# One layer of attention, RWKV-7 and PEER experts on one core: which token blocks gather their experts' rows, and which pair is retrieved jointly

## The chip, the cores and the metric

The kernel runs on one core of a Trainium2 chip. The metric is the device time of one execution, in microseconds. Engines are called TensorE (PE in the rows; PEld are its weight loads), VectorE (DVE), ScalarE (ACT), GpSimd (POOL) and SyncE (SP). SP issues the plain transfers, POOL the gathers.

## The reference

For 512 tokens of width 1024, in float32, the layer computes an input projection, eight heads of latent attention with a block-causal mask, eight heads of RWKV-7 time mixing (a recurrence over the tokens), an output projection with residual, and a PEER layer over 16384 experts. Only the last part is touched by the change. In short:

```python
h = rms_norm(x, g_ffn)
q = (h @ w_pq).reshape(TOK_BLOCK, 8, 2, 128)
s = einsum('thpd,hpnd->thpn', q, sub_keys)          # 8 heads, 2 halves, 128 keys each
s1, i1 = top_k(s[:, :, 0], 16); s2, i2 = top_k(s[:, :, 1], 16)
top_s, pos = top_k(all sums s1 + s2, 16)            # 16 experts per head: 128 per token
idx = i1 * 128 + i2 of these;  gate = softmax(top_s)
act = gelu(einsum('thkd,td->thk', expert_u[idx], h))
x = x + einsum('thk,thkd->td', gate * act, expert_v[idx])
```

## The kernel before, in words

The 512 tokens are four blocks (0 to 3) of 128. Each block goes through stages: F (front, norm and input projection), R (chunks, the parallel part of RWKV), M (latent, attention), S (scan, the recurrence, which needs S of the block before) and B (back). B holds the output projection (`out_proj`, L792), the norm (`norm_ffn`), the retrieval (`retrieve`: queries by L848, scores by L855, the best 16 by `top16`, L825 to L835, all on VectorE) and the route (`route`: the best 16 of the sums, and the experts' indices, L925). A block's S ends with its output `yT` (L782).

The program is unrolled. A loop at the end of the function writes the stages' pieces in the order in which they would run side by side, by costs given per stage; five lanes (R, M, S, B, late F) share buffers and banks within a lane. `BACK` says in which items the lane of B goes through the blocks: there (0), then (1, 2) jointly, then (3). A joint item streams the weights once for two blocks, with matmuls of 256 columns in the queries instead of 128. The tile framework then orders the instructions of each engine when the program is built: an instruction that stands earlier in the text goes first where two are ready, and a later one may run as soon as its inputs and buffers are there. Each engine works its own list off in order.

The experts of a block are computed in one of two ways:

- `GATHERED` blocks (`experts`, L969 to L996): for each of the 128 experts of a token, GpSimd issues an indirect DMA that fetches one 4 KB row of `expert_u` per partition (L978) into one of `GA` = 4 buffers `ga`; VectorE multiplies it with the token and sums (L988), and ScalarE takes the gelu by groups of 32. Then the same for `expert_v`, whose rows VectorE adds up in `acc` (L991). That is 256 gathers and 256 VectorE instructions per block; the groups of v of one stand between those of u of the next group.
- `DENSE` blocks (`dense`): their 256 tokens go through all 16384 experts, 128 to a tile. `up(e)` (L1103 as float32, or L1117 as three exact products of parts that ScalarE and VectorE split off, L1063 and L1064) gives activations. `gate_half` gives the gates, in 32 steps of eight tokens for each half of the experts: VectorE makes B (L1035, L1036), ScalarE makes A (eight instructions L1039 and one L1040), TensorE multiplies (L1043), ScalarE stores (L1048). `down(e)` multiplies activations with gates (L1134) and adds up the output in PSUM (L1138 as float32, L1149 in parts). At most 16 tiles of activations wait on chip and 12 more in DRAM, so 28 run before the first step down, which needs the gates of all tokens.

The dense part's tokens come from DRAM (`h2d`), written by `norm_ffn` of the dense blocks; a gathered block's `norm_ffn` transposes back and stores `h2r` instead. Block 1's first projections are kept in two of the buffers `ga`, which are idle then (`EARLY`).

The lines at the change are these, before:

```python
BACK = [("F", (0,)), ("F", (1,)), ("B", (0,)), ("B", (1, 2)), ("B", (3,))]
GATHERED = (0, 3)
DENSE = (1, 2)
...
    early.close()
    dense()
    for b in GATHERED:
        experts(b, *routed[b])
```

Of the kernel before, what the change touches and what calls it, by code (L numbers as in the profile page):

```python
# [29 lines left out]
TOPK = 16  # L30
# [4 lines left out]

# columns of the packed per-channel vectors
CV = {}
# [5 lines left out]
NCV = _n  # L43
# columns of the packed per-feature rows
RV = {}
# [4 lines left out]
NRV = _n  # L50
# candidate pairs (a, b) of the two sorted lists that can be among the best 16 sums, in order of a * 16 + b:
# (a, b) has (a + 1) * (b + 1) - 1 pairs before it that are at least as large
RUNS = [(a, TOPK // (a + 1)) for a in range(TOPK)]
NCAND = sum(n for _, n in RUNS)

# lanes of stages: buffers, banks and weight tiles (count, width) of each
LANE = {"R": 1, "M": 2, "S": 4, "F": 3, "B": 3}
# [4 lines left out]
PM = 7  # L62
BACK = [("F", (0,)), ("F", (1,)), ("B", (0,)), ("B", (1, 2)), ("B", (3,))]
# blocks whose tokens gather their experts' rows, blocks that go through all experts
GATHERED = (0, 3)
DENSE = (1, 2)
EARLY = 1
GROUP, GA = 32, 4
# dense blocks: gates of HALF * 128 experts at a time, in GBUFS tiles of SUB * 128; activations run AHEAD tiles ahead,
# FIRST of them before the first gates, KEPT more wait in DRAM  # L70
HALF, SUB, GBUFS = 64, 16, 5
FIRST, AHEAD, KEPT = 12, 16, 12
# [4 lines left out]
def u_whole(e):  # L77
    """float32 products of four passes, where the vector engine has no time to split; else three exact parts"""
    return e < 28 or 47 <= e - AHEAD < 64
# [7 lines left out]
def layer_kernel(ctx: ExitStack, tc: tile.TileContext, x, pos, cvec, rvec, w_mla, w_rwkv, w_uq, w_ukv, lora, g2,  # L87
# [4 lines left out]
    dp = ctx.enter_context(tc.tile_pool(name="dp", bufs=1, space=bass.MemoryType.DRAM))  # L92
    # what the last block's tail needs lies apart: its pools outlive those of the other stages
    pools, psums = {}, {}
    last = ctx.enter_context(ExitStack())
    pools[3] = last.enter_context(tc.tile_pool(name="wb", bufs=1, side="right"))
    psums[3] = last.enter_context(tc.tile_pool(name="psb", bufs=1, space=PSUM, side="right"))
    # the tail takes over the buffers of the second lane
    pools[2] = ctx.enter_context(tc.tile_pool(name="wm", bufs=1))
# [10 lines left out]
    lane = [3]  # L110
# [28 lines left out]

    # ---------------------------------------------------------------- constants  # L140
    def load_x(b):
# [55 lines left out]
    for b in LEVELS:  # L197
# [7 lines left out]
        lmask[b] = m  # L205
    # rows (beta s | kappa s), columns (alpha t | rho t)
    mmask = cst([P, 2, C], "mmask")
# [50 lines left out]

    # rotary tables, token-major
    posi = cst([P, NB], "posi", I32)  # L260
# [12 lines left out]
    for i, ph in ((0, 0.25), (1, 0.0)):  # L273
# [3 lines left out]
        src = ang  # L277
        for c in TWO_PI:
            V.scalar_tensor_tensor(red, kr, -c, src, op0=OP.mult, op1=OP.add)
            src = red  # L280
# [29 lines left out]
    def square_sum(src, scr, acc):  # L310
        """the squares go to a tile that is written after them"""
        act(scr, src, AF.Square, accum_out=acc)

    def head_squares(src, n, acc, h0=0):
        """acc[:, h0 + i] = sum of squares of src[:, i, :n]"""
        for i in range(src.shape[1]):
            act(sb([P, QK], "hscr", dt=BF16)[:, :n], src[:, i, :], AF.Square, accum_out=acc[:, h0 + i:h0 + i + 1])

    # ---------------------------------------------------------------- stages
    def norm_in(xt, hT, carry):  # L320
        """channel-major normalized tokens, after the last one of the block before"""
        ss = sb([P, 1], "ss", 2)
        square_sum(xt.rearrange("p (a b) -> p a b", a=KC), hT[:, :, 1:], ss)
        r = rstd(ss, 1, 1.0 / D, EPS, "nx")
        act(xt, xt, AF.Copy, scale=r)
        if carry is None:
            V.memset(hT[:, :, 0:1], 0.0)
        else:
            V.tensor_copy(hT[:, :, 0:1], carry)
        for i in range(2):  # L330
            p = bank()
            for j in range(4):
                nc.tensor.transpose(p[:, j * P:(j + 1) * P], xt[:, (4 * i + j) * P:(4 * i + j + 1) * P], ident)
            for j in range(4):
                act(hT[:, 4 * i + j, 1:P + 1], p[:, j * P:(j + 1) * P], AF.Copy, scale=col("g_mix", 4 * i + j))
            yield
        carry = sb([P, KC, 1], "carry", 2)
        V.tensor_copy(carry, hT[:, :, P:P + 1])
        return carry

    def rwkv_in(b, hT):
        pm = {}
        if b == EARLY:
            # the gather's buffers are idle until the first block's experts are known
            t = [gb([P, D], "ga", GA).rearrange("p (a b) -> p a b", b=P) for _ in range(2)]
            pm = {"k": t[0][:, 0:4], "r": t[0][:, 4:8], "v": t[1][:, 0:4], "x": t[1][:, 4:6]}
        for g, cols in (("x", (12, 13)), ("k", range(4, 8)), ("r", range(4)), ("v", range(8, 12))):
            if b != EARLY:
                pm[g] = sb([P, 4, P], "pm", PM, pool=wa) if len(cols) == 4 else sb([P, 2, P], "px", 2, pool=wa)
            for i, c in enumerate(cols):  # L350
                w = wtile(w_rwkv[c])
                p = bank()
                for kc in range(KC):
                    mm(p[:, :P + 1], w[:, kc, :], hT[:, kc, :], start=kc == 0, stop=kc == KC - 1)
                t = pm[g][:, i, :]
                act(t, p[:, 1:P + 1], AF.Copy, scale=ommu[:, c:c + 1])
                V.scalar_tensor_tensor(t, p[:, 0:P], col("mu", c), t, op0=OP.mult, op1=OP.add)
                yield
        return pm

    def mla(b, hT, yT):
# [30 lines left out]
        yield  # L392
        # queries
        qs = sb([P, H], "qs")
# [30 lines left out]
        yield  # L425
        # keys and values
        kps, vps = bank(), bank()
# [24 lines left out]
        if b + 1 < NB:  # L452
            nc.sync.dma_start(vd[b], vb)
        # block-causal attention, four heads at a time
        nk = (b + 1) * P
# [72 lines left out]
    def rwkv_chunks(b, pm):  # L528
# [67 lines left out]
        yield  # L596
        # bonus weight and gate
        rk = r
# [6 lines left out]
        yield  # L605
        # values, token-major
        UV = [med(H, C) for _ in range(2)]
# [15 lines left out]
        yield  # L623
        # chunk-local products
        MT, BKt = [], []
        for c in range(2):
# [9 lines left out]
            yield  # L636
        # inverse of the unit lower triangular systems: two chunks stacked on the partitions, heads side by side
        for s in range(2):
# [15 lines left out]
        for c in range(2):  # L654
# [3 lines left out]
            t = med(4, P)  # L658
# [49 lines left out]
    def rwkv_scan(b, AR, BKt, MT, UV, YF, wc, bv, sg, yT):  # L708
        # the recurrence over chunks
        yt = med(H, C)  # L710
        for c in range(2):
# [4 lines left out]
            rows = slice(c * C, (c + 1) * C)  # L716
# [40 lines left out]
            yield  # L757
        # group norm, bonus, gate
        mean = sb([P, H], "mean")
# [64 lines left out]
    def top16(items):  # L824
        """items: (values, indices, source); the chains of several items interleaved"""  # L825
        for (v, i, src) in items:
# [10 lines left out]
    def retrieve(bs, h2T):  # L837
        """the best TOPK of both halves' keys, per block"""
        nb = len(bs)
# [22 lines left out]
    def route(b, tv, ti):  # L862
        yield
        # the lists of indices as steps: what each rank adds to the one before
        tf = ti.bitcast(F32)
# [11 lines left out]
        a = 0  # L877
        while a < TOPK:
            n = RUNS[a][1]
# [13 lines left out]
        for g in range(2):  # L893
            top16([(top[:, h], pi[:, h], cs_[:, h]) for h in range(4 * g, 4 * g + 4)])
            yield
        # rank a of the first list from a candidate's place, rank b of the second from its place within the run
        pf = pi.bitcast(F32)
# [40 lines left out]
        for i, (src, sc) in enumerate(ranks):  # L938
            if b in DENSE:
                summed(p[:, i * P:(i + 1) * P], stepped(src), sc, True)  # L940
            else:
                n = TOPK
# [85 lines left out]
    def gate_half(dn, g, parts):  # L1028
        """gates of experts i1 * 128 + i2, i1 in one half: [i2, sub, token, i1 of the SUB]; parts: what takes each run
        of subs"""  # L1030
        i1T, i2T, gT = slots
# [20 lines left out]
    def dense():  # L1052
# [8 lines left out]
        def split(t, hi, lo):  # L1061
            """two parts of a float32 tile that the one-pass products carry whole"""
            act(hi, t, AF.Copy)  # L1063
            V.tensor_tensor(lo, t, hi, op=OP.subtract)  # L1064
# [10 lines left out]
        hs = []  # L1075
        # room for activations in the buffers of the second lane
        room = [("q", 1, 3), ("k", 1, 3)] + [("wst", WST[2][0], 3)] * WST[2][0]
# [13 lines left out]
        def up(e, keep=False):  # L1091
            """activations of the experts of a tile, for all tokens of these blocks"""
            if e in kept:
# [89 lines left out]

    # stages of the blocks, emitted in the order in which they would run side by side; what runs in one lane shares
    # its buffers
    stages = {"F": (front, 16, 32), "R": (chunks, 24, 110), "M": (latent, 46, 95), "S": (scan, 10, 28),
# [10 lines left out]
    while any(lanes):  # L1197
# [19 lines left out]
        try:  # L1217
# [5 lines left out]
            lanes[i].pop(0)  # L1223
            running[i] = None
    early.close()
    dense()
    for b in GATHERED:
        experts(b, *routed[b])

# [57 lines left out]
```

## Time and profile before

| | us |
|---|---|
| median of 3 runs | 1783.02 |
| lowest, highest | 1781.82, 1790.86 |
| span of the profiled execution, first to last instruction | 1781.3 |
| TensorE matmul / weight load busy | 1651.5 / 1394.3 |
| VectorE / ScalarE / GpSimd busy | 1334.4 / 932.6 / 702.6 |
| mean granted TensorE clock | 0.950 |

The profile is of one execution. It gives the span and no other time for it; its span lies 1.7 us under the median of the runs. Busy times are unions of an engine's instructions; a matmul's end is modelled, and successive matmuls overlap in it. L12 is line 12 of the kernel. "out<-in" names what an instruction writes and reads, "x" counts the instructions of a group.

### The profile page before, as it was taken

The page shows a single profiled execution, that of the slowest core. Times are in us where ns is not written, and L with a number is a line of the kernel's source. Part 1 is how long each engine was busy: PE and PEld are TensorE (multiplying, and loading weights), DVE is VectorE, ACT ScalarE, POOL GpSimd, SP SyncE. Part 2 cuts the span into 40 slices and gives each one's busy share as a digit, 9 for nine tenths or more (in the row PEclk, how much of TensorE's full clock was granted, in tenths as well). Part 3 has the DMA queues.
Part 4 walks back from the last instruction along what each step waited for, and adds up shares of the span by engine and source line. Part 5 has one row for each costly group of instructions (what it writes and reads, how often), then busy time and mean ns, then how long its engine had stood idle before and what let it go on. Part 6 is the DMA issues. An engine that isn't in the chain of part 4 may idle for free. (4 is left out here: it accounts for less than half of the span.)

```text
span 1781.3 us, 29137 instructions
## 1 busy us (share of the span) xinstructions
PE 1651.5 (93%) x10183; PEld 1394.3 (78%) x10183; DVE 1334.4 (75%) x2987; ACT 932.6 (52%) x2465; POOL 702.6 (39%) x562
## 2 busy tenths in 40 slices
PE   7999999998999998788997899999999999999987
PEld 6897799787867987567995577888777778888864
DVE  3412414775586789887789789998887799999898
ACT  5656454644545332367774334444768645445443
POOL 1001100244554444454443253334455446356453
PEclk9998999997697999988999999999989999999999
DMA  7634565596689988789997799998989999999988
GB/s 272 196 122 135 164 233 194 203 337 223 213 309 329 324 321 294 290 283 310 364 331 250 258 359 352 359 355 325 327 312 319 312 343 351 366 318 371 346 293 330
DMA packets 154866, 520.71 MB, mean 292 GB/s; under 512 B 17312, under 2 KB 24096, under 8 KB 154720
## 3 DMA queue, kind: packets, MB, share of 16 engines
q0 software_dynamic: 73728, 268.47, 43.1%
q1 hardware_dynamic: 80992, 250.39, 39.6%
q8 instruction: 80, 1.31, 0.3%
q14 instruction: 66, 0.54, 0.1%
HBM read 508.96 MB, written 9.83 MB: 291 GB/s over the span
## 5 line engine op out<-in xcount | busy, mean ns | idle before, releaser
L978 POOL DMA_INDIRECT ga<-in_expert_v_dram,idx x256 | 352.3, 1376 | 381.7 <-DVE acc L991 285.5
L978 POOL DMA_INDIRECT ga<-in_expert_u_dram,idx x256 | 299.8, 1171 | 372.0 <-DVE ga L988 257.5
L991 DVE SCALAR_TENSOR_TENSOR acc<-ga,dots,acc 128x1024 f32<-128x1024 f32 x256 | 327.9, 1281 | 65.9 <-DMA ga<-in_expert_v_dram,idx 64.9
L988 DVE SCALAR_TENSOR_TENSOR ga<-ga,h 128x1024 f32<-128x1024 f32 x256 | 311.6, 1220 | 52.3 <-DMA ga<-in_expert_u_dram,idx 52.1
L1149 PE MATMUL po<-xh,t 128*128 128x512 f32 x880 | 307.7, 407 | 12.7 <-DVE t L1064 5.7
L1117 PE MATMUL ps<-dh,ul 128*128 128x256 f32 x664 | 191.1, 288 | 7.9 <-DVE ul L1064 7.4
L1149 PEld LDWEIGHTS po<-xh,t 128*128 128x128 f32 x880 | 159.6, 192 | 48.6 <-ACT xh L1063 13.2
L1117 PE MATMUL ps<-dh,uh 128*128 128x256 f32 x664 | 189.8, 286 | 6.5 <-ACT uh L1063 6.5
L1149 PE MATMUL po<-xl,t 128*128 128x512 f32 x440 | 179.6, 408 | 14.6 <-DVE xl L1064 14.2
L1117 PE MATMUL ps<-dl,uh 128*128 128x256 f32 x664 | 187.5, 282 | 0.0
L1063 ACT ACTIVATE xh<-v 128x512 fp32r<-128x512 f32 x220 | 134.6, 626 | 96.4 <-PE po L1149 73.9
L1103 PE MATMUL ps<-t,u 128*128 128x256 f32 x720 | 172.6, 393 | 9.1 <-DMA u<-in_expert_ut_dram 8.8
L1103 PEld LDWEIGHTS ps<-t,u 128*128 128x128 f32 x720 | 138.5, 197 | 32.3 <-issue 6.3
L1064 DVE TENSOR_TENSOR xl<-v,xh 128x512 fp32r<-128x512 f32 x220 | 147.7, 690 | 16.2 <-ACT xh L1063 15.7
L1043 PEld LDWEIGHTS ps<-B,A 128*128 128x128 f32 x1024 | 131.3, 204 | 35.3 <-ACT ge L951 10.6
L1039 ACT ACTIVATE A<-iotap,slots 128x128 f32<-128x128 f32 x512 | 156.1, 395 | 0.0
L1043 PE MATMUL ps<-B,A 128*128 128x64 f32 x1024 | 131.5, 285 | 23.6 <-DVE B L1036 10.4
L1063 ACT ACTIVATE uh<-u 128x512 fp32r<-128x512 f32 x166 | 98.5, 625 | 83.8 <-PE ps L1117 52.0
L1117 PEld LDWEIGHTS ps<-dh,ul 128*128 128x128 f32 x664 | 126.4, 190 | 17.3 <-DVE ul L1064 13.4
L1117 PEld LDWEIGHTS ps<-dh,uh 128*128 128x128 f32 x664 | 126.4, 190 | 17.1 <-ACT uh L1063 10.0
L1117 PEld LDWEIGHTS ps<-dl,uh 128*128 128x128 f32 x664 | 126.4, 190 | 3.5 <-issue 0.7
L848 PE MATMUL ps<-h2T,wst 128*128 128x128 f32 (+1 forms) x768 | 125.1, 318 | 3.1 <-DMA wst<-in_w_pq_dram 3.1
(402 smaller groups left out, 2924.1 us busy)
## 6 DMA issues: line engine op xcount, KB each, us to landing
u<-in_expert_ut_dram SPq DMA_DIRECT2D x128, 512.0 KB, 6.7
v<-in_expert_v_dram SPq DMA_DIRECT2D x128, 512.0 KB, 6.6
wst<-in_w_rwkv_dram SPq DMA_DIRECT2D x56, 512.0 KB, 4.4
wst<-in_w_pq_dram SPq DMA_DIRECT2D x48, 512.0 KB, 6.7
wst<-in_w_o_dram SPq DMA_DIRECT2D x24, 512.0 KB, 5.2
wst<-in_w_mla_dram SPq DMA_DIRECT2D x16, 336.0 KB, 3.9
t<-in_x_dram SPq DMA_DIRECT2D x8, 512.0 KB, 4.6
wst<-in_w_ukv_dram SPq DMA_DIRECT2D x16, 256.0 KB, 3.5
```

Of the source, the lines that this page charges most:

```text
L848: mm(p[:, :nb * P], w[:, kc, :], h2T[:, kc, :], start=kc == 0, stop=kc == KC - 1)
L978: G.indirect_dma_start(out=t, out_offset=None, in_=table, in_offset=bass.IndirectOffsetOnAxis(ap=idx[:, j:j + 1], axis=0))
L988: V.scalar_tensor_tensor(u, u, 1.0, h2, op0=OP.mult, op1=OP.mult, accum_out=dots[:, j:j + 1])
L991: V.scalar_tensor_tensor(acc, row_of(expert_v, j), dots[:, j:j + 1], acc, op0=OP.mult, op1=OP.add)
L1039: act(A[:, j, :], iotap, AF.Abs, scale=-1.0, bias=i2T[:, t0 + j:t0 + j + 1])
L1043: mm(p[:, j * HALF:(j + 1) * HALF], A[:, j, :], B[:, j, :], start=True, stop=True)
L1063: act(hi, t, AF.Copy)
L1064: V.tensor_tensor(lo, t, hi, op=OP.subtract)
L1103: mm(p, u[:, kc, :], hd[kc // 2][:, kc % 2, :], start=kc == 0, stop=kc == KC - 1)
L1117: mm(p, a[:, k, :], h[:, kc, :], start=kc + i == 0, stop=kc == KC - 1 and i == 2)
L1149: mm(po[i][n], ww[:, i * P:(i + 1) * P], vv, start=e + k == 0, stop=e == P - 1 and k == 2)
```

## The change

Blocks 0 and 1 gather, blocks 2 and 3 go through all experts. The lane of B goes through (0), (1) and then (2, 3) jointly. The gathered blocks' `experts` stand before `dense` in the text, and before the buffers of the early stages are released. The diff also takes comments out, which is left away here.

```diff
-BACK = [("F", (0,)), ("F", (1,)), ("B", (0,)), ("B", (1, 2)), ("B", (3,))]
+BACK = [("F", (0,)), ("F", (1,)), ("B", (0,)), ("B", (1,)), ("B", (2, 3))]
...
-GATHERED = (0, 3)
-DENSE = (1, 2)
+GATHERED = (0, 1)
+DENSE = (2, 3)
...
+    for b in GATHERED:
+        experts(b, *routed[b])
     early.close()
     dense()
-    for b in GATHERED:
-        experts(b, *routed[b])
```

## Rows read from the trace of the kernel before

**Rows 1.** The page: busy us, share of the span and instructions by engine.

```profile
PE 1651.5 (93%) x10183; PEld 1394.3 (78%) x10183; DVE 1334.4 (75%) x2987; ACT 932.6 (52%) x2465; POOL 702.6 (39%) x562
```

**Rows 2.** One line's instructions, L782, 600 to 800: ns min/median/max, first and last start.

```profile
L782 DVE TENSOR_TENSOR yT<-t,ps x1: 689/689/689, 733.7 to 733.7; 128x512 f32<-128x512 f32 x1
```

**Rows 3.** Busy us by stretch: length, PE, PEld, DVE, ACT, POOL, clock, DMA share, GB/s.

```profile
0.00:484.00 484.00, 461.30 (x3366) 400.19 (x3366) 215.04 (x716) 264.31 (x829) 97.84 (x91) 0.93 0.63 207
484.00:734.00 250.00, 232.12 (x1309) 190.42 (x1308) 197.03 (x585) 100.08 (x293) 122.43 (x107) 0.92 0.90 314
734.00:957.00 223.00, 197.67 (x1242) 173.00 (x1239) 189.59 (x532) 154.84 (x408) 96.17 (x83) 0.92 0.89 316
957.00:1781.00 824.00, 760.38 (x4273) 630.67 (x4271) 732.79 (x1159) 413.35 (x938) 386.15 (x282) 0.98 0.91 329
```

**Rows 4.** The gathers, L978: by line; POOL in 439:539; groups in 957:1781 (idle, releasers).

```profile
L978 POOL DMA_INDIRECT ga<-in_expert_u_dram,idx x256: 933/1086/3800, 338.7 to 1676.2; - x128
L978 POOL DMA_INDIRECT ga<-in_expert_v_dram,idx x256: 932/1152/6302, 433.9 to 1766.6; - x128
...
439.00:539.00 100.00, 44.73 (x39) 0.78 0.77 261
...
L978 POOL DMA_INDIRECT ga<-in_expert_v_dram,idx x154 | 234.3, 1522 | 228.3 <-DVE acc L991 191.8 <-DVE ga L988 10.0 <-DMA ga<-in_expert_v_dram,idx 6.4
L978 POOL DMA_INDIRECT ga<-in_expert_u_dram,idx x128 | 151.8, 1186 | 200.0 <-DVE ga L988 168.6 <-DMA ga<-in_expert_v_dram,idx 17.7 <-issue 7.6
```

**Rows 5.** Groups of PE: blocks 1 and 2 (484 to 690), then block 3 (756 to 947).

```profile
L848 PE MATMUL ps<-h2T,wst 128*128 128x256 f32 x256 | 59.3, 385 | 2.3 <-DMA wst<-in_w_pq_dram 2.3
L792 PE MATMUL ps<-wst,yT 128*128 128x512 f32 x52 | 23.9, 598 | 0.0
...
L848 PE MATMUL ps<-h2T,wst 128*128 128x128 f32 x256 | 34.1, 291 | 0.0
L792 PE MATMUL ps<-wst,yT 128*128 128x512 f32 x32 | 15.2, 604 | 0.2 <-DVE t L796 0.2
```

**Rows 6.** Lines L792 (block 3) and L848 (block 3; 1 and 2; 0).

```profile
L792 PE MATMUL ps<-wst,yT x32: 592/592/697, 782.6 to 811.4; 128*128 128x512 f32 x32
L848 PE MATMUL ps<-h2T,wst x256: 272/275/527, 843.0 to 920.6; 128*128 128x128 f32 x128
L848 PE MATMUL ps<-h2T,wst x256: 379/379/741, 580.9 to 676.5; 128*128 128x256 f32 x128
L848 PE MATMUL ps<-h2T,wst x256: 273/275/348, 242.4 to 300.2; 128*128 128x128 f32 x128
```

**Rows 7.** First half of the gates: line L1035, groups of ACT (756 to 947), line L1138.

```profile
L1035 DVE TENSOR_TENSOR B<-iotap,slots x32: 672/685/698, 756.1 to 931.9; 128x512 f32<-128x512 f32 x32
...
L1039 ACT ACTIVATE A<-iotap,slots 128x128 f32<-128x128 f32 x246 | 75.1, 392 | 0.0
L1040 ACT ACTIVATE A<-A 128x1024 f32<-128x1024 f32 x32 | 33.6, 1054 | 0.3
L1048 ACT ACTIVATE G<-ps 128x512 f32<-128x512 f32 x31 | 18.3, 591 | 18.9 <-PE ps L1043 18.8
...
L1138 PE MATMUL po<-v,q x16: 592/592/1055, 953.6 to 970.0; 128*128 128x512 f32 x16
```

**Rows 8.** The timeline in the tail: start, us, instruction.

```profile
1639.23 0.39 PE L1149 MATMUL po<-xh,t 128*128 128x512 f32 x1
1639.46 0.39 PE L1149 MATMUL po<-xl,t 128*128 128x512 f32 x1
1639.46 0.19 PEld L1149 LDWEIGHTS po<-xh,t 128*128 128x128 f32 x1
1639.69 0.39 PE L1149 MATMUL po<-xh,t 128*128 128x512 f32 x1
```

**Rows 9.** The last stretch (columns as in rows 3); a piece of the chain that ended last.

```profile
1700.00:1782.00 82.00, 66.03 (x283) 46.48 (x281) 70.52 (x94) 29.99 (x56) 40.82 (x26) 0.97 0.88 310
...
1723.89 8.38 DMA ga<-in_expert_v_dram,idx
```

## The prediction

> **What bounds the kernel now.** I read the page's busy times first. TensorE is busy 93% of the span, VectorE 75%, ScalarE 52% [rows 1], so TensorE comes first; but the kernel has several stages, and I looked for where one ends. The front (RWKV, attention, the first retrievals) reaches to the last result of the last scan, at 733.7 + 0.7 = 734.4 us [rows 2]. From 734 to 957 the retrieval of block 3 runs beside the first half of the gates and 28 tiles of activations. From 957 on the dense tail runs: 128 steps down, the other activations, the second half of the gates. TensorE idles 23 + 18 us in the two stretches of the front, 25 in the third, 64 in the tail [rows 3]. No stretch has a large hole, because each wait on one chain is covered by matmuls of another. That cover is what the change moves.
>
> Then the gathers. They run from 338.7 to 1766.6 us, though the program's text puts them last [rows 4]: a place in the text ranks instructions, it does not time them. They go at 39 rows per 100 us early, where VectorE has room, and at 282 rows in the 810 us from 957 on, 35 per 100; GpSimd meanwhile waits most of its idle time for VectorE to free a row's buffer [rows 4]. So the gathers are a second chain, about as long as the kernel, and room on VectorE barely speeds them up.
>
> **The change part by part.** No work is added or removed. Before and after there are two gathered and two dense blocks, two single retrievals and one joint one, three sweeps over the weights of the output projection and of the queries, 512 gathered rows, 128 expert tiles of each table. With the blocks, eight transposes and one 512 KB store of block-major rows go from block 3 to block 1, and the store of transposed rows goes the other way. So SP, GpSimd and TensorE issue the same; what stands beside what is different. The edited comments cost nothing.
>
> Moved: (a) block 1's retrieval runs alone, as soon as scan 1 is done, in the front; (b) the joint retrieval, now of blocks 2 and 3, waits for scan 3 and has nothing of the front beside it; (c) the dense part needs block 3 and so stands behind (b), where before it waited for blocks 1 and 2 only; (d) the gathers rank above the dense part, not below it. The wait that (c) adds is that of four loads on SP for the store of block 3's normed rows; behind them in SP's order stand the loads of expert tiles, and behind those TensorE's activations. The weights of the late retrieval rank ahead of them, so nothing else is held.
>
> *End of the front.* The joint retrieval's queries kept TensorE busy 59.3 us, its output projection 23.9 for 52 recorded of 64 matmuls, 29.4 for all. The single ones of block 3 took 34.1 and 15.2 [rows 5]. A single one in the front's place saves 59.3 + 29.4 - 34.1 - 15.2 = 39 us of a nearly full TensorE: the front ends at 734 - 39 = 695. Bounds: 734, if the scans' own chain sets it; 654, if the front has no idle left at all (693 busy us to 734 [rows 3], less 39).
>
> *Front to joint queries.* Nothing of the front covers this now. Block 3 needed 60 us from its first matmul of the output projection (782.6) to its first of the queries (843.0) [rows 6]. I take 60, and 50 from below, since more work stood in its way then. Joint queries at 755.
>
> *Queries to first gates.* Before, 580.9 to 756.1 = 175 us [rows 6, 7]. In the first 96 of them (to 676.5) the queries used 59.3 of TensorE and the scores' products a little more; the rest, some 28, went to blocks that are now done. VectorE's sorting and gathers stay. I take 175 - 28 = 147; the ends are 175 and 96, the time in which block 0 alone went from its first query (242.4) [rows 6] to its first gather (338.7) [rows 4]. First gates at 902. The activations of 28 tiles cover a part of TensorE's wait while VectorE routes. There are only 28 before the first step down, so they run out.
>
> *First gates to first step down.* All 32 steps of the half must be done, as each step down reads all tokens. On ScalarE a step costs 8 x 0.392 + 1.054 + 0.591 = 4.78 us, 32 of them 153. Before, it took 197.5 (756.1 to 953.6) [rows 7], with block 3's retrieval ahead of it on every engine; that one is gone. I take 153 and one step more to fill the pipe, 158; bounds 153 and 198. First step down: 902 + 158 = 1060, against 953.6: 106 us later.
>
> By TensorE's account: the 891 us of work that rows 3 give to 957 would now spread over 1060, with 169 idle instead of 66. Idle can also bring the clock down: where TensorE was busy 198 of 223 us, its granted clock averaged 0.92 of 2.4 GHz, where it was busy 760 of 824 us 0.98 [rows 3]. So some of this work may run at 1.2 GHz. I give that no term of its own; the upper ends hold it.
>
> *The tail.* Before: 953.6 to 1781.3 = 828. Its inner loops run without gaps: matmuls of 512 columns follow one another every 0.23 us [rows 8]. The last 82 us are different: TensorE is busy 66, and VectorE holds the final steps because it stands, in order, behind gathered rows, one of which took 8.4 us to land [rows 9]. After the change 230 + 0.39 x 103 = 270 rows are gathered by 1060 (512 - 282 = 230 by 957 [rows 4]); the last 242 need 620 to 700 us at 39 to 35 per 100, so the gathers end at 1680 to 1760, well before the dense part. I take 82 - 66 = 16 us off: 812. Bounds: 828 (rows of a higher rank hold VectorE as much as they give back) and 788 (half of the other 48 us of idle is filled as well).
>
> The Trainium skill would read the tail otherwise: "Perfetto Trace Analysis", section "Identifying the Most-Contended Engine", holds that a busy matmul row is no measure of headroom and takes weight-load busy time instead. By that the tail, at 631 of 824 us, has a quarter to spare, and with VectorE freed the tail could fall far below 788. The trace differs: with 512-column matmuls 0.23 us apart and one weight load of 0.19 to each [rows 8], the loads of the steps down can't fill more than 0.19 / 0.23 = 83%.
>
> Sum: 695 + 60 + 147 + 158 + 812 = 1872 us of span. The profiled span is 1781.3; the median of the runs is 1.7 above it, and no other time of the profiled execution is given. With 1.7: **1874 us**, 5% slower.
>
> **The rivals.** *Faster: the tail is not TensorE's.* If gathered rows held VectorE and so TensorE, and their rank above the dense part cleared them early, the tail could run at the pace of its weight loads, 631 us [rows 3]. Then 1060 + 631 + 2 = 1693. It decides once the tail is under 712. For it: a gather's transfer stands in the chain that ended last [rows 9]. Against: the spacing, and that rows go no faster than 39 per 100 us where VectorE has room. 0.05.
>
> *No change: the route hides.* If the front ends at 654 and the late retrieval goes as block 0's did, the first step down comes at 654 + 60 + 96 + 153 = 963 and the end at 963 + 812 + 2 = 1777. Against: block 0 had one block's sorting and no gathers on VectorE. 0.05.
>
> *Slower by little.* The front at 654, first gates after 125, the rest as I have it: 654 + 60 + 125 + 158 + 812 + 2 = 1811. 0.1.
>
> *Slower by more: nothing shrinks.* 734 + 60 + 175 + 198 + 828 + 2 = 1997. There is little reason for all of it, but half of the way goes past 1930. 0.1.
>
> **How the numbers follow.** My case has 0.7, between 1815 and 1930; the time is its sum. The range 1815 to 1930 cuts through the last two cases and leaves out the first two, about 0.2 in all. A measurement of this kernel tells about 0.5% (9 us) from no change: faster 0.05, same 0.05, slower 0.9.
>
> **What would show it.** The last scan's last result at 670 to 715 us; the joint queries 60 us on; the first gates near 902; the first step down near 1060; some 100 us more of holes in TensorE, nearly all between the end of the front and the first step down; no gathers in the last 100 us. A first step down before 980 would break the main step. A tail under 780 with the step at its place would show that VectorE and not TensorE set the tail's pace; one over 840, that the gathers' higher rank takes from the dense part.

## The result, and the profile after

The changed kernel takes 1901.4 us (median of 4, 1897.7 to 1903.8) against 1782.4: a ratio of 1.067, 95% interval 1.062 to 1.072. The forecast was 1874 us, in a range from 1815 to 1930. The profiled execution has a span of 1900.9 us, 119.6 more than before.

The page of the kernel after, busy times and three of its rows in 40 slices, against [rows 1]:

```profile
PE 1675.9 (88%) x10183; PEld 1418.9 (75%) x10183; DVE 1345.2 (71%) x2987; ACT 935.5 (49%) x2463; POOL 707.3 (37%) x562
...
PE   7999999998988857990689677999998998999998
...
POOL 1001100445545565345465544444445556700000
PEclk9998999998986668995688788999998999999999
```

The same instructions run, in the same numbers on TensorE, VectorE and GpSimd. What is new is the hole in TensorE's row in the middle, the lower clock around it, and a tail whose last slices have no gathers.

The stretches of the kernel after (columns as in rows 3), cut where the last scan ends, at the first gates and at the first step down:

```profile
0.00:484.00 484.00, 459.14 (x3413) 396.40 (x3414) 218.79 (x723) 264.89 (x828) 95.28 (x93) 0.96 0.67 225
484.00:690.00 206.00, 178.07 (x1098) 153.73 (x1097) 167.47 (x447) 81.72 (x253) 110.58 (x94) 0.77 0.85 283
690.00:920.00 230.00, 148.32 (x627) 112.73 (x626) 171.40 (x578) 35.89 (x92) 111.25 (x93) 0.80 0.87 306
920.00:1099.00 179.00, 145.21 (x821) 131.28 (x821) 147.79 (x253) 140.29 (x362) 102.78 (x77) 0.81 0.84 285
1099.00:1901.00 802.00, 745.21 (x4228) 624.78 (x4228) 639.70 (x991) 412.71 (x929) 287.37 (x207) 0.97 0.81 289
```

TensorE idles 82 us from 690 to 920 and 34 from there to 1099, against 25 in the third of rows 3. From 484 to 1099 its granted clock averages 0.77 to 0.81 of 2.4 GHz, against 0.92 in the second and third of rows 3, so a larger part of its work runs at 1.2 GHz; its busy time grows by 24 us though it does the same. These 24 us and 95 of idle are the 119. The clock does not follow the idle share here: it is lowest from 484 to 690, where TensorE is busy 178 of 206 us.

The lines that carry the forecast's steps, kernel after (duration min/median/max in ns, first and last start), for [rows 2, 4, 6, 7]:

```profile
L782 DVE TENSOR_TENSOR yT<-t,ps x1: 683/683/683, 689.5 to 689.5; 128x512 f32<-128x512 f32 x1
L848 PE MATMUL ps<-h2T,wst x256: 379/379/796, 746.7 to 845.1; 128*128 128x256 f32 x128
L1035 DVE TENSOR_TENSOR B<-iotap,slots x32: 672/684/689, 919.7 to 1073.9; 128x512 f32<-128x512 f32 x32
L1138 PE MATMUL po<-v,q x16: 590/592/697, 1100.0 to 1114.3; 128*128 128x512 f32 x16
L978 POOL DMA_INDIRECT ga<-in_expert_u_dram,idx x256: 932/950/3134, 343.7 to 1557.9; - x128
L978 POOL DMA_INDIRECT ga<-in_expert_v_dram,idx x256: 932/1144/5838, 436.9 to 1661.0; - x128
```

| step, us | forecast | after | off |
|---|---|---|---|
| end of the last scan | 695 | 690.2 | -4.8 |
| to the joint queries | 60 | 56.5 | -3.5 |
| to the first gates | 147 | 173.0 | +26.0 |
| to the first step down | 158 | 180.3 | +22.3 |
| tail | 812 | 800.9 | -11.1 |
| span | 1872 | 1900.9 | +28.9 |

Read as one chain the two kernels are almost alike. Before, the later dense block was block 2; its scan ended at 525.6, and the first step down came 428.0 us later, at 953.6 [rows 7]:

```profile
L782 DVE TENSOR_TENSOR yT<-t,ps x1: 678/678/678, 524.9 to 524.9; 128x512 f32<-128x512 f32 x1
```

(this is line L782 of the kernel before, from 460 to 530). After, it is block 3, whose scan ends at 690.2, and the first step down comes 409.8 us later. The start of the chain moved by 164.6 us, the chain is 18.2 shorter, the tail 26.8: 164.6 - 18.2 - 26.8 = 119.6, the whole difference. This is a sum of stretches; what sets each of them the runs below have to show, and for the kernel before they do not show it.

What fills the chain shows in who waited for whom in the kernel after, 740 to 1100 (us in total, times, longest), and in the one hole of 45 us in TensorE's timeline:

```profile
PEld L911 <- DVE t L919: 45.8, 1, 45.8
...
DVE ga L988 <- DMA ga<-in_expert_u_dram,idx: 35.2, 25, 3.7
DVE acc L991 <- DMA ga<-in_expert_v_dram,idx: 25.5, 20, 4.4
```

```profile
849.80 0.94 PE L855 MATMUL ps<-wst,t 128*128 128x128 f32 x7
850.59 4.05 PE L1103 MATMUL ps<-t,u 128*128 128x256 f32 x18
900.05 1.33 PE L911 MATMUL ps<-t,identb 128*128 128x128 bf16 x8 [45.41 <-DVE t L919]
```

TensorE has done the scores and 12 tiles of activations by 855 and then waits for VectorE's route (`route`, the choice among the sums). VectorE itself waits 61 us in this stretch, in its order, for rows of the gathers to land: a gathered row's instruction stands between the instructions of the sorting and holds those behind it.

### The profile page after: what moved, and what is told of

Its sections match the earlier page's. It is cut to its first block, busy times and chain, and to the rows that moved or that the text cites. A ratio compares the mean times of both kernels' runs of the same rounds, so it can differ in the third digit from the quotient of the medians.

```text
span 1900.9 us, 29241 instructions
## 1 busy us (share of the span) xinstructions
PE 1675.9 (88%) x10183; PEld 1418.9 (75%) x10183; DVE 1345.2 (71%) x2987; ACT 935.5 (49%) x2463; POOL 707.3 (37%) x562
## 4 chain that ended last, share of the span: by engine, by line
PE 47%; DMA 20%; issue 12%; DVE 12%; POOL 8%; ACT 1%; SPq 0%; POOLq 0%; DVEq 0%; ACTq 0%
PE po L1149 11%; DMA ga<-in_expert_v_dram,idx 10%; PE ps L1117 9%; POOL ga L978 8%; PE ps L354 5%; DMA ga<-in_expert_u_dram,idx 5%; PE ps L848 3%; DVE ga L988 3%; DVE acc L991 3%; PE ps L792 2%; PE ps L674 1%; PE ps L365 1%; PE ps L631 1%; PE ps L690 1%; DMA wst<-in_w_o_dram 1%
## 5 line engine op out<-in xcount | busy, mean ns | idle before, releaser
L978 POOL DMA_INDIRECT ga<-in_expert_v_dram,idx x256 | 361.9, 1414 | 321.7 <-DVE acc L991 226.2
L978 POOL DMA_INDIRECT ga<-in_expert_u_dram,idx x256 | 292.3, 1142 | 310.0 <-DVE ga L988 192.2
L1149 PE MATMUL po<-xh,t 128*128 128x512 f32 x880 | 303.1, 401 | 10.0 <-DVE t L1064 7.3
L1103 PE MATMUL ps<-t,u 128*128 128x256 f32 x720 | 176.8, 401 | 0.0
L1063 ACT ACTIVATE uh<-u 128x512 fp32r<-128x512 f32 x166 | 103.4, 628 | 139.9 <-PE ps L1117 108.8
L1043 PE MATMUL ps<-B,A 128*128 128x64 f32 x1024 | 135.6, 294 | 38.3 <-DVE B L1036 14.5
L1103 PEld LDWEIGHTS ps<-t,u 128*128 128x128 f32 x720 | 143.0, 203 | 22.0 <-issue 1.4
L1064 DVE TENSOR_TENSOR ul<-u,uh 128x512 fp32r<-128x512 f32 x166 | 113.4, 689 | 49.9 <-ACT uh L1063 34.8
L848 PE MATMUL ps<-h2T,wst 128*128 128x128 f32 (+1 forms) x768 | 124.2, 318 | 9.4 <-DMA wst<-in_w_pq_dram 9.0
```

Source lines behind the costliest of these rows:

```text
L848: mm(p[:, :nb * P], w[:, kc, :], h2T[:, kc, :], start=kc == 0, stop=kc == KC - 1)
L978: G.indirect_dma_start(out=t, out_offset=None, in_=table, in_offset=bass.IndirectOffsetOnAxis(ap=idx[:, j:j + 1], axis=0))
L1043: mm(p[:, j * HALF:(j + 1) * HALF], A[:, j, :], B[:, j, :], start=True, stop=True)
L1103: mm(p, u[:, kc, :], hd[kc // 2][:, kc % 2, :], start=kc == 0, stop=kc == KC - 1)
L1149: mm(po[i][n], ww[:, i * P:(i + 1) * P], vv, start=e + k == 0, stop=e == P - 1 and k == 2)
```

## The experiments

Four theories were tested: that the rank of the gathers costs; that TensorE's lost cover is the loss (the forecast's own words); that VectorE's sorting and the gathers in its order pace the late retrieval; that ScalarE paces the gates. The letters of the theories are those of each expectation, which says what it means by them. Stages below are in us of each run's profile, taken from the same lines as above.

**The rank alone**, in the changed kernel put back, and in the kernel before put in:

```diff
+    early.close()
+    dense()
     for b in GATHERED:
         experts(b, *routed[b])
-    early.close()
-    dense()
```

> The changed kernel with the gathered blocks' experts put back behind the dense part in the text, all else as changed. Theory A (the loss is the stretch from the last scan to the first step down, because the dense part needs block 3; the rank of the gathers is worth nothing): 1890 to 1910 us, first step down within 15 us of 1100, the gathers end later than 1662. Theory B (rows of a higher rank take VectorE from the late retrieval and the gates): under 1870 us, first step down before 1070.

Measured: 1895.8 us, ratio to the kernel before 1.065 (1.061 to 1.069). First gates at 912.6, first step down at 1096.6; the gathers end at 1654.5, not later as expected. Put back, the rank changes nothing that can be told from noise (the intervals of the two ratios overlap).

> The kernel before with only the experts of its gathered blocks (0 and 3) put ahead of the dense part in the text. Theory A (rank is worth nothing): within 1% of the kernel before, 1765 to 1800 us. Theory B (a higher rank takes VectorE from the dense part): 1810 us or more. If rank shortens the tail by itself: under 1765 us.

Measured: 1770.1 us, ratio 0.996 (0.993 to 0.999). The last scan and the first step down stay where they were (734.0 and 951.2); the tail is 812.4 us instead of 827.7. The time lies in theory A's range. So in the kernel before the rank by itself is a small gain, about half a per cent, and the loss belongs to the choice of the blocks and the order of their retrieval that goes with it. This is the one version that came out ahead of both kernels.

**Blocks 2 and 3 one after the other** instead of jointly:

```diff
-..., ("B", (2, 3))]
+..., ("B", (2,)), ("B", (3,))]
```

> The changed kernel with blocks 2 and 3 retrieved one after the other instead of jointly. Theory A (missing cover): block 2's retrieval runs beside the last scan and its sixteen steps of the gates beside block 3's retrieval, so the first step down comes at 1010 to 1050 instead of 1100, 1815 to 1860 us in all, in spite of one more sweep of the weights. Theory C (what costs is that block 3 comes last at all, joint or not): 1885 us or more.

Measured: 1860.5 us, ratio 1.043 (1.037 to 1.049), just over the top of theory A's range. The lines L848, L1035 and L1138 of this run:

```profile
L848 PE MATMUL ps<-h2T,wst x512: 272/275/582, 642.8 to 865.8; 128*128 128x128 f32 x171
L1035 DVE TENSOR_TENSOR B<-iotap,slots x32: 675/683/695, 768.7 to 1023.5; 128x512 f32<-128x512 f32 x32
L1138 PE MATMUL po<-v,q x16: 592/592/1222, 1046.2 to 1060.5; 128*128 128x512 f32 x16
```

Block 2's queries start at 643, ahead of scan 3's end at 690.1, and its gates at 769. The first step down comes 54 us earlier than in the changed kernel, in spite of one more sweep of the weights. So of the 119 us some 41 are the joint item's; the rest stays when block 3 comes last by itself. The Trainium skill ("Perfetto Trace Analysis", section "Optimization Strategy") says that interleaving stretches in which different engines are the most contended may help; this run agrees, with its 41 us.

**TensorE's hole filled.** All 28 tiles of activations ahead of the gates in the text:

```diff
-FIRST, AHEAD, KEPT = 12, 16, 12
+FIRST, AHEAD, KEPT = 28, 16, 12
...
         for e in range(FIRST):
-            up(e)
+            up(e, e >= AHEAD)
```

> The changed kernel with all 28 tiles of activations written ahead of the gates in the text instead of 12, so that they fill the hole in which TensorE had nothing at 855 to 900 us. Theory A (TensorE's idle in that stretch is the loss): the 16 other tiles, some 60 us of TensorE, leave the stretch of the gates, which then runs at ScalarE's 153 us: first step down at 1065 to 1085, 1865 to 1890 us in all. Theory D (the gates wait for VectorE's sorting and are then set by ScalarE whatever TensorE does): first step down within 10 us of 1100, 1893 us or more.

Measured: 1894.3 us, ratio 1.065 (1.061 to 1.069), not told apart from the change itself. Its stretches, last scan to first gates and first gates to first step down:

```profile
688.00:914.00 226.00, 191.00 (x825) 148.36 (x825) 173.71 (x596) 40.55 (x106) 105.42 (x93) 0.93 0.94 341
914.00:1091.00 177.00, 139.25 (x642) 128.91 (x641) 154.67 (x247) 137.02 (x349) 105.92 (x85) 0.60 0.84 281
```

The hole is gone: TensorE is busy 191 of 226 us instead of 148 of 230. Yet both stretches keep their length, and in the second, now with 642 matmuls instead of 821, TensorE's clock is down to 0.60 and its busy time hardly falls. Nor is it this clock that holds the second stretch: in it ScalarE waited 6 us in all for the products of the gates, in the changed kernel 13 (its line first):

```profile
ACT G L1048 <- PE ps L1043: 12.8, 14, 2.6
...
ACT G L1048 <- PE ps L1043: 5.8, 5, 1.7
```

TensorE's idle was not what cost the time; theory D's numbers hold.

**The store of the normed rows after the queries,** meant to keep the activations out of the queries' way:

```diff
-        if b in DENSE:
-            i = DENSE.index(b)
-            nc.sync.dma_start(h2d[:, :, i * P:(i + 1) * P], h2T)
...
         lists = yield from retrieve(bs, h2T)
+        for i, b in enumerate(bs):
+            if b in DENSE:
+                j = DENSE.index(b)
+                nc.sync.dma_start(h2d[:, :, j * P:(j + 1) * P], h2T[:, :, i * P:(i + 1) * P])
```

> The changed kernel with the store of blocks 2 and 3's normed rows, for which the activations wait, moved behind the joint queries: the twelve tiles of activations then can't stand between the queries and fall into the hole at 855 to 900 us. Theory T (the activations slow the queries and with them all that follows): queries done in 65 to 80 us instead of 99, first gates 20 to 35 us earlier, 1865 to 1885 us in all. Theory V (VectorE's sorting sets the pace): queries done sooner, first gates within 10 us of 920, 1890 to 1905 us.

Measured: 1903.6 us, ratio 1.069 (1.065 to 1.073). The queries took 95.7 us from first to last start instead of 98.4, the first gates came at 915.0. But the edit did not move what it was meant to move. The store and the activations among the queries, in the changed kernel and then in this run, whose line numbers are shifted (the store's first and last start; TensorE's group from 746 to 846 and from 749 to 846):

```profile
L822 SPq DMA_DIRECT2D h2d<-h2T x2: 513/558/603, 741.7 to 747.7; - x2
L1103 PE MATMUL ps<-t,u 128*128 128x256 f32 x162 | 36.8, 379 | 0.0
...
L1025 SPq DMA_DIRECT2D h2d<-h2T x2: 513/558/603, 745.6 to 750.6; - x2
L1104 PE MATMUL ps<-t,u 128*128 128x256 f32 x161 | 36.6, 379 | 0.0
```

The store went out 3 to 4 us later, beside the first queries, as its place in the text only ranks it; as many matmuls of activations as before stand among the queries. So the run decides nothing between theories T and V, though the time is the one that V gave.

**The gathers left out:**

```diff
     for b in GATHERED:
-        experts(b, *routed[b])
+        acc = gb([P, D], "acc")
+        nc.sync.dma_start(acc, x2d[b])
+        nc.sync.dma_start(out[b * P:(b + 1) * P, :], acc)
```

> The changed kernel with the experts of blocks 0 and 1 left out (their rows of the output are only the residual; 512 gathers and 512 instructions of VectorE go). Theory V (after the front VectorE's sorting, shared with the gathers, sets the late retrieval's pace): from the first joint query to the first gates 110 to 140 us instead of 173. Theory T (TensorE's queries, with the activations between them, set it): 160 us or more. The tail, if it is TensorE's own: 780 to 800 us instead of 801; if the gathers held it: under 770.

Measured once: 1715.3 us. Queries to first gates, first gates to first step down, and the tail:

```profile
693.00:817.00 124.00, 114.40 (x553) 96.78 (x553) 60.12 (x431) 21.69 (x53) 0.00 (x0) 0.93 0.39 131
817.00:974.00 157.00, 139.47 (x811) 126.38 (x812) 58.70 (x137) 135.13 (x353) 0.00 (x0) 0.85 0.20 67
...
974.00:1713.00 739.00, 725.49 (x4240) 622.52 (x4239) 404.29 (x689) 421.35 (x936) 0.00 (x0) 0.99 0.49 164
```

Queries to gates: 124 us instead of 173, in the middle of theory V's range, with 60 us of VectorE in place of 138. The two parts of this stretch, up to the last query and from there to the first gates, in the changed kernel and then in this run, and VectorE's costliest wait in this run from 693 to 817 (us, times, longest):

```profile
747.00:846.00 99.00, 97.40 (x466) 85.76 (x466) 70.88 (x246) 15.26 (x37) 41.57 (x36) 0.98 0.94 336
846.00:920.00 74.00, 17.47 (x89) 11.69 (x87) 66.96 (x286) 8.65 (x22) 37.74 (x31) 0.59 0.73 241
...
693.00:780.00 87.00, 87.00 (x422) 77.09 (x423) 28.34 (x192) 14.04 (x32) 0.00 (x0) 0.99 0.46 157
780.00:817.00 37.00, 27.40 (x132) 19.70 (x130) 31.78 (x239) 7.65 (x21) 0.00 (x0) 0.78 0.21 71
...
DVE tv L827 <- ACT t L857: 70.9, 4, 28.7
```

Up to the last query TensorE is full in both runs, with queries and activations; there the gathers cost 11 us. Behind it the stretch is VectorE's, 67 busy us of 74; there they cost 38. Without them VectorE waits 71 us for scores, so TensorE's queries set most of what is left. Gates to first step down: 160 instead of 180, close to ScalarE's 153. The tail: 737 instead of 801, under the 770 that stood for "the gathers held it". With 512 gathers less each stage shrinks: the front by 29, the way to the queries by 25, then 49, 20 and 64 us, 187 in all. The run takes away VectorE's work, the waits for landing rows, and half of the transfers (DMA share 0.49 in the tail instead of 0.81); which of these counts most was not tried.

**ScalarE's part of the gates cut:**

```diff
-            for j in range(8):
-                act(A[:, j, :], iotap, AF.Abs, scale=-1.0, bias=i2T[:, t0 + j:t0 + j + 1])
+            for j in range(0, 8, 2):
+                act(A[:, j:j + 2, :], bm(iotap, 2), AF.Abs, scale=-1.0, bias=i2T[:, t0 + j:t0 + j + 1])
```

> The changed kernel with ScalarE's part of the gates cut: four instructions of twice the width per step instead of eight, each with one token's index for two tokens, so every other token's gates are another token's. Theory D (ScalarE sets the stretch of the gates): at 0.39 and perhaps 0.5 us a piece a step goes from 4.8 to 3.7 us, so 32 steps lose 35 us: from the first gates to the first step down 140 to 155 us instead of 180, 1855 to 1880 us in all. Rival (VectorE and the wait for block 3's route set it): 170 us or more.

Measured once: 1862.8 us. Groups of ScalarE's instructions from 919 to 1064, and the first gates and first step down of this run:

```profile
L1039 ACT ACTIVATE A<-iotap,slots 128x256 f32<-128x256 f32 x132 | 56.0, 500 | 0.0
L1040 ACT ACTIVATE A<-A 128x1024 f32<-128x1024 f32 x34 | 34.1, 1049 | 0.1
...
L1035 DVE TENSOR_TENSOR B<-iotap,slots x32: 666/683/687, 919.2 to 1047.1; 128x512 f32<-128x512 f32 x32
...
L1138 PE MATMUL po<-v,q x16: 592/592/1222, 1064.5 to 1081.1; 128*128 128x512 f32 x16
```

A wide instruction took 500 ns, a step 3.6 us, and the stretch 145.3 instead of 180.3: 35 us off, as worked out from ScalarE's durations. The whole kernel followed. ScalarE sets this stretch.

**Both cuts together:** the single items and the wide instructions, with every other token's gates replaced as above.

> Two cuts of the chain from the last scan to the first step down together: blocks 2 and 3 retrieved one after the other, and ScalarE's part of the gates cut to four wide instructions per step (every other token's gates are another token's). If both stand on one chain, one behind the other, their gains add: with the first alone the first step down came at 1046, and 28 of the 32 steps stood at the end of its chain, so 28 x 1.1 = 31 us off: 1005 to 1025, and with the second half's steps 1815 to 1835 us in all. If one hides the other: 1845 us or more.

Measured: 1838.8 us, ratio 1.033 (1.025 to 1.040), between the two. The first step down came at 1031.7: 15 of the 31 us arrived. In the run with single items alone the fifth step of the gates starts only at 879, after block 3's queries (866), so its later steps hang on more than ScalarE; what holds them was not tried. So the two gains add only in part.

**Three more kernels, towards a faster version.** First, the kernel before with the higher rank and all activations ahead of the gates.

> The kernel before with both edits that did not hurt: the experts of the gathered blocks ahead of the dense part in the text, and all 28 tiles of activations ahead of the gates. Theory A: the rank is worth the 0.4% that it gave alone; the activations have no hole to fill before (no idle stretch of TensorE above 11 us), so nothing more: 1765 to 1785 us. If the order of the activations helps by itself: under 1760 us.

Measured: 1820.5 us, ratio 1.022 (1.020 to 1.025), outside both ranges. The first step down came at 999.2 instead of the 951.2 with the rank alone. Where there was no hole, 16 more tiles ahead of the gates pushed the gates back: from the first gates to the first step down 231.7 us instead of 197.0. TensorE was busy 204 of these us at a granted clock of 0.79, so in the kernel before, what TensorE does ahead of the gates counts.

Then A of the gates from GpSimd, for the changed kernel and for the kernel before with the higher rank, computing the same:

```diff
-            for j in range(8):
-                act(A[:, j, :], iotap, AF.Abs, scale=-1.0, bias=i2T[:, t0 + j:t0 + j + 1])
+            G.tensor_tensor(A, bm(iotap, 8), bc(i2T[:, t0:t0 + 8], P), op=OP.subtract)
+            act(A, A, AF.Abs)
             act(A, A, AF.Relu, scale=-1.0, bias=1.0)
```

> The changed kernel with the gates' A made from one subtraction by GpSimd over eight tokens and two wide instructions of ScalarE, in place of eight narrow and one wide one; the result is the same. ScalarE's step goes from 4.78 to 2 x 1.05 + 0.59 = 2.7 us. Theory D (ScalarE sets the stretch of the gates): from the first gates to the first step down 110 to 150 us instead of 180, 1825 to 1875 us in all. Rival (the subtraction waits in GpSimd's order behind gathers and becomes the pace): 180 us or more, 1890 us or more.

> The kernel before with the experts of the gathered blocks ahead of the dense part in the text and the gates' A made by GpSimd and ScalarE as in the run beside it. If the chain from the dense blocks' last scan through the gates sets the first step down in the kernel before too, it comes at 890 to 935 us instead of 951, 1710 to 1755 us in all. If TensorE, filled by block 3's retrieval there, sets it: 1760 to 1775 us, as with the rank alone.

Measured: 1952.1 us, ratio 1.095 (1.090 to 1.100), and 1849.8 us, ratio 1.037 (1.033 to 1.042). The first is what its rival said, with 201.7 us from the first gates to the first step down; the second lies outside both ranges. The subtraction in the first of them, and who waited for it:

```profile
L1038 POOL TENSOR_TENSOR A<-iotap,slots x64: 1893/1916/3925, 913.2 to 1602.5; 128x1024 f32<-128x1024 f32 x64
...
  ACT A L1039: 127.7, 53
```

It takes 1.9 us, and ScalarE waited 128 us for it: it stands in GpSimd's order among the gathers, each of which waits for a buffer. The first step down came at 1119.7, and the gathers, held up in turn, ended at 1767 instead of 1662. The second run, in which first gates to first step down took 223 us, says nothing on what ScalarE's share was worth in the kernel before.

## Why the prediction was right, and where not

*End of the front*, 695: 690.2. 44 us came instead of 39, but that TensorE's time sets this end is not shown. With block 2 retrieved by itself TensorE had more to do before this end, 189 busy us and 1300 matmuls from 484 to 690 against 178 and 1098, and the last scan ended at 690.1 all the same:

```profile
484.00:690.00 206.00, 189.08 (x1300) 161.03 (x1300) 164.85 (x489) 90.20 (x284) 100.91 (x85) 0.88 0.89 307
```

(that run; the changed kernel's row stands above). Without the gathers it ended 29 us earlier. So the size was right partly by luck, and the cause of this end stays open.

*To the joint queries*, 60: 56.5. Block 3's row was a fair measure in length only. The output projection needs a block's attention as well as its scan, and after the change block 3's attention is the later of the two (the last step of its output, L524, before and after):

```profile
L524 ACT ACTIVATE yT<-ps,cv x4: 350/354/359, 682.3 to 683.1; 128x128 f32<-128x128 f32 x4
...
L524 ACT ACTIVATE yT<-ps,cv x4: 360/367/376, 701.3 to 702.1; 128x128 f32<-128x128 f32 x4
```

So the projection goes on only at 701.8, 12 us behind the scan's end, and the queries follow 45 us later, where the forecast's row had 60. The wait for the attention was not in the sum; it and the shorter way behind it cancelled. Without the gathers the whole took 31.

*To the first gates*, 147: 173.0, as long as the 175 of before. This term was mis-sized. I took 28 us off because TensorE no longer served other blocks there. It still served something: 37 us of the dense part's activations, which I had set beside VectorE's route, stand among the queries, so these took 98 us from first to last start, as the 96 before, with TensorE busy 97 of 99. The 75 us behind them (80 before) are VectorE's sorting with gathered rows among it, which take 37 without the gathers. Filling TensorE's hole behind the queries gained 2 us. Whether queries without the activations would bring the gates forward was not tested.

*To the first step down*, 158: 180.3. ScalarE as the pace was right (35 us less when its instructions were cut, 160 us without the gathers); that the gathers add some 20 to it was not in the sum.

*The tail*, 812: 800.9. It is 27 us shorter, not 16, and only 9 of them lie at its end: the last 82 us hold 75 us of TensorE's work instead of 66, and hold no more without any gathers (the changed kernel, then that run):

```profile
1818.90:1900.90 82.00, 74.90 (x384) 63.27 (x382) 47.37 (x83) 39.44 (x77) 0.00 (x0) 0.98 0.49 166
1631.50:1713.50 82.00, 75.06 (x385) 63.39 (x384) 47.48 (x83) 39.44 (x77) 0.00 (x0) 0.97 0.50 166
```

So 16 was too much for the end, and the other 18 us had no term. That the tail is TensorE's own was too strong: the bound of 788 was worked out from its idle time, and without gathers it took 737, so the gathers held 64 us of it. The Trainium skill's measure that I weighed ("Perfetto Trace Analysis", section "Identifying the Most-Contended Engine"), weight loads at 77%, did point to room; its size, down to 631, did not come: at 737 the loads fill 84% and TensorE is busy 98%.

*Cover* as the cause was the wrong word. What I called TensorE's lost cover is real as idle, but filled it is worth nothing. In the changed kernel the chain from the end of block 3's scan and attention sets the first step down: TensorE, full up to the last query, then VectorE to the first gates, then ScalarE in the gates. The change moved its start by 165 us. That one chain sets it in the kernel before too (428 us there, 410 here) is a reading of the sum only: there more activations ahead of the gates cost 48 us, so TensorE counts as well. The sum came out right in size because each term was taken as a stretch of that chain, and also because misses cancelled: two terms were 48 us too short, three 19 too long.

*The clock.* The forecast's remark that idle can bring the clock down is not borne out as a rule here: 0.77 with TensorE busy 178 of 206 us, 0.80 with 148 of 230. That some of the work would run at 1.2 GHz came true.

Of the rivals, "faster" needed a tail under 712, and even without gathers it took 737; "no change" and "slower by little" needed a shorter chain, "slower by more" a front that didn't shrink. None came, though of the last one the stretch to the first gates did not shrink. The gathers ended at 1662, 18 us ahead of my 1680 to 1760, and went at 40 rows per 100 us up to the first step down (305 rows from 344 to 1099), close to the 39 that I held to be their pace.

## What to carry to other kernels

When a change decides which piece of work comes last, follow the latency chain from that piece's last input to the first instruction of the longest stage, engine by engine, and shift its start; the busiest engine's idle time can be a result of that chain, and filling it need not give anything back. Transfers whose consumers stand in the same engine's order as a latency-bound chain can lengthen that chain, by their work and by each late landing; here they cost 49 us on the way to the first gates and 20 in the gates. An idle engine is no place for a step of such a chain if its own order is full of waits, as GpSimd's was. And where a place in the text only ranks, a run that moves a line is a test only if its trace shows that the instructions moved.

## What the runs showed of the hardware

GpSimd's subtraction of 128x1024 float32 took 1.92 us, and each of the two wide ScalarE instructions behind it 1.06; the eight narrow ones that they replaced took 3.13 together. A ScalarE instruction of twice the width took 500 ns instead of 391. With TensorE's hole filled, its granted clock fell to a mean of 0.60 of 2.4 GHz, most of it at 1.2 GHz, over 177 us in which it was busy 139, with matmuls of 64 columns between waits, while it was 0.93 in the 226 us before, busy 191.
